# A hybrid decoder layer on one core: the meta tokens' state from one stacked product, two scan outputs in one step, and moving rows placed at the weights' address modulo 256

## The chip, the cores and the metric

The kernel runs on one core of a Trainium2 chip. A core has a matrix engine (TensorE, "PE" in the profile; its weight loads are listed apart as "PEld"), a vector engine (VectorE, "DVE"), an activation engine (ScalarE, "ACT"), a general engine (GpSimd, "POOL") and a queue engine (SyncE, "SP"), each working through its own list of instructions in order, and DMA engines that move data from the chip's main memory. The metric is the device time of one execution in microseconds (us). Three runs of the kernel before gave a median of 1025.13 us, from 1024.91 to 1025.34.

## The reference

One decoder layer works on 512 positions of width 1024, with 16 learned "meta" positions put in front (528 in all; the 16 are dropped at the end). After a normalization, one wide projection makes the inputs of two branches that run side by side, and their gates:

```python
u = rmsnorm(h, mix_norm_w[i])
proj = u @ w_in[i]                      # pool inputs, z, x/B/C, dt, gates
y_pool = pool_mixer(u_pool, pool_w_group[i], pool_scale[i]) @ w_pool_up[i]
y_ssd = mamba2_branch(z, xbc, dt_raw, ...) @ w_ssd_out[i]
h = h + (gate_pool * y_pool + gate_ssd * y_ssd) @ w_o[i]
v = rmsnorm(h, mlp_norm_w[i])
hid = jax.nn.relu(v @ w_ff1[i])
h = h + (hid * hid) @ w_ff2[i]
out = rmsnorm(h, final_norm_w)[:, N_META:]
```

The Mamba-2 branch has 32 heads of width 64 in 8 groups of 4; B and C (128 states) are shared by a group. It runs over chunks: the 16 meta tokens are a partial chunk of their own, and four chunks of 128 follow.

```python
y_diag = einsum(cb * lmat, x*dt)                       # inside a chunk
states = einsum("bclgn,bclgr,bcgrpn", b, decay, x*dt)  # one state per chunk
h_next = chunk_decay * h + states                      # from chunk to chunk
y_off  = einsum(c, h, exp(a_cs))                       # what earlier chunks bring in
y = (y_diag + y_off + x * d_skip) * silu(z)            # then a norm per group
```

The change touches how the meta chunk's state (16 positions, 128 states, 4 heads of 64) is computed, how `y_off` and `y_diag` of the two halves of a group are ordered, and where some operands lie in the on-chip memory.

## The kernel before, in words

**Precision.** Most products run with both factors split in two: `hi` is the float32 number rounded to the matrix engine's faster float32r format, `lo` the rest, and three products (hi·hi, hi·lo, lo·hi) are added up in PSUM. So each weight block of 128 x 1024 is fetched by SP's queue (`raw`, L72), copied to `whi` by ACT (L73), and its rest `wlo` is made by DVE (L74). Some small products are left in plain float32, which the matrix engine takes in two passes (two records in the trace): the chunks' products `pcb`, `pst`, `po` and `py`.

**Projections.** `proj` (L143, L144, L146) walks over eight k-steps. `narrow` projections (z, gates) use moving rows of 512 positions, 24 matmuls a block. `wide` ones (x, B, C, pooled inputs), which also need the meta tokens, move two runs of 258, 260 or 264 positions, 48 matmuls a block. The moving rows are the split `u` (`uh`, `ul`; before the norm is known, `xh`, `xl`), kept as tiles of 64 + 512 floats whose last 528 are used: a narrow slice starts 64 floats into its tile, a wide one 48.

**The scan.** For each group g, `ssd(g)` is a generator of seven steps: transposes (`ptb`, `ptm`, `ptx`) and the decayed inputs (`xdt`, `xdd`; for the meta tokens `xdtm`, `xddm`); then `pcb` and the state products `pst`, the first of them (L449) over the 16 meta tokens, which DVE chains from chunk to chunk (`st`, L455 and L456); then one step for each of the two 128-row halves (`po` at L464, `py` at L470, four DVE instructions); then three steps for the group's norm. `group_proj(g + 1)` is a generator of the next group's projections: `bt` (`px` 16 + g), `ct` (24 + g), two of `xc` (2g, 2g + 1), sometimes a gate, then `pz`. `weave` takes the two in turn, one step of each.

**What sets the order.** Each engine executes a fixed list in order. The lists are not simply the order of the source: when the program is built, a planner orders each engine's list by its own estimate of when inputs are ready, so parts of `po` stand between matmuls of a projection. A wait at the head of a list holds everything behind it on that engine. `px`, `pz` and the like share two PSUM buffers of two banks (`psa`); the scan's tiles share four of one bank (`psb`), so a buffer has to be read out before its second successor can start.

**Later stages**, which the change touches only by where `u` and the pooled rows lie: the pooling branch, the gates, the up-projection, the output projection `w_o` and the MLP, both of the latter with sums of quarter blocks.

Of the kernel before, what the change touches and what calls it, by code (L numbers as in the profile page):

```python
# [9 lines left out]
F32 = mybir.dt.float32  # L10
F32R = mybir.dt.float32r
AF = mybir.ActivationFunctionType
ALU = mybir.AluOpType

P = 128
D = 1024
SEQ = 512
NM = 16
# [3 lines left out]
G = 8  # L22
R = 4
HEADS = 32
DI = 2048
FF = 4096
EPS = 1e-5
# [16 lines left out]

WO_ORDER = [(q, i) for q in ("b11", "b12", "b22") for i in range(2)]
WARM = 9


@with_exitstack
def kernel(ctx: ExitStack, tc, xT, x, w, vec, fnw, out):  # L50
    nc = tc.nc
    act, dve, pe, pool = nc.scalar, nc.vector, nc.tensor, nc.gpsimd
# [45 lines left out]
    ones_f = const.tile([P, P], F32, name="ones_f")  # L98
# [13 lines left out]
    def col(off, i, n=P):  # L112
        return vs[:n, off + i : off + i + 1]

    dtok = const.tile([P, 2, 4, HEADS], F32, name="dtok")
    dtm = const.tile([NM, 2, HEADS], F32, name="dtm")
    dec = const.tile([P, 4, HEADS], F32, name="dec")
    cdec = const.tile([P, 4, HEADS], F32, name="cdec")
    decm = const.tile([NM, HEADS], F32, name="decm")

    u_stack = ExitStack()
    up = u_stack.enter_context(tc.tile_pool(name="up", bufs=1, side="left"))

    up.tile([P, 16], F32, name="u_pad")
    uh = [up.tile([P, 64 + SEQ], F32R, name=f"uh{k}")[:, 64 - NM :] for k in range(NK)]
    ul = [up.tile([P, 64 + SEQ], F32R, name=f"ul{k}")[:, 64 - NM :] for k in range(NK)]

    gc_stack = ExitStack()
    gc = gc_stack.enter_context(tc.tile_pool(name="gc", bufs=2, side="left", reuse_waits="tile"))
    m1p = ctx.enter_context(tc.tile_pool(name="m1p", bufs=1, side="right", reuse_waits="tile"))  # L130
    m1 = [m1p.tile([P, SEQ], F32, tag=f"m1_{d}", name=f"m1_{d}") for d in range(NK)]

# [3 lines left out]
    def psum1(name):  # L136
        return psb.tile([P, 512], F32, tag="s", name=name)
# [25 lines left out]
    pre = pre_stack.enter_context(tc.tile_pool(name="pre", bufs=1, side="right"))  # L163
# [1 line left out]

    xh = [pre.tile([P, 64 + SEQ], F32R, name=f"xh{k}")[:, 64 - NM :] for k in range(NK)]
    xl = [pre.tile([P, 64 + SEQ], F32R, name=f"xl{k}")[:, 64 - NM :] for k in range(NK)]
    pre.tile([P, 24], F32, name="x_pad")
    rsb = pre.tile([P, L], F32, name="rsb")
    q = pre.tile([P, L], F32, name="q")  # L170
    X, U = (xh, xl), (uh, ul)
    H = HEADS

# [7 lines left out]
    b, raw, hi, lo = wdt  # L181
# [3 lines left out]

    for n in range(WARM):
        pe.matmul(pdt[1].rearrange("p (a b) -> p a b", a=4), ones_r,
# [65 lines left out]
    for t, name in ((rsh, "dgh"), (rsl, "dgl")):  # L253
        d = pre.tile([NT, 6, NT], F32R, tag="sq", name=name, bufs=2)
# [3 lines left out]
    for i in range(2):  # L258
        pb = psum1(f"pb1_{i}")
        c = slice(3 * i, 3 * i + 3)  # L260
        for n in range(2):
            pe.matmul(pb[:, : 3 * NT], ones_r[:NT], dg[n][:, c, :].rearrange("p a b -> p (a b)"),
                      start=n == 0, stop=n == 1)
# [11 lines left out]
    for c in range(4):  # L275
        r = slice(c * H, (c + 1) * H)
# [27 lines left out]
    for j, src in enumerate((dt, acs)):  # L304
# [6 lines left out]
              start=True, stop=True)  # L311
# [5 lines left out]
    act.activation(decm, decm, AF.Exp)  # L317
    act.activation(fl(cdec), pq[:, :128], AF.Exp)


    def norm_u():
        for k in range(NK):
            dve.scalar_tensor_tensor(xt[k], xt[k], col(V_MIX, k), rsb, op0=ALU.mult, op1=ALU.mult)
            act.copy(uh[k], xt[k])
            dve.tensor_tensor(ul[k], xt[k], uh[k].bitcast(F32), op=ALU.subtract)
# [54 lines left out]
    def bc(ap, n):  # L380
        return ap.unsqueeze(len(ap.shape)).to_broadcast(list(ap.shape) + [n])

    def ssd(g, cur):

        xc, bt, ct, zt = cur
        hs = slice(R * g, R * g + R)
        tok = lambda c: slice(NM + c * P, NM + (c + 1) * P)
        ctok = lambda c: slice(c * P, (c + 1) * P)
        flat = lambda t: t.rearrange("p r d -> p (r d)")
# [1 line left out]
        nc.gpsimd.dma_start(abc, acs_d[hs, :].partition_broadcast(P))  # L391

        xdt = gs.tile([P, 4, R, 64], F32, tag="xdt", name=f"xdt{g}")
        xdtm = gs.tile([NM, R, 64], F32, tag="xdtm", name=f"xdtm{g}")
        btok = gs.tile([P, 3, P], F32, tag="btok", name=f"btok{g}")
        btm = gs.tile([NM, P], F32, tag="btm", name=f"btm{g}")
        ptb = psum1(f"ptb{g}")
        for c in range(3):
            pe.transpose(ptb[:, c * P : (c + 1) * P], bt[:, tok(c)], ident)
        pe.transpose(ptb[:NM, 3 * P :], bt[:, :NM], ident)  # L400
        act.copy(btok.rearrange("p c n -> p (c n)"), ptb[:, : 3 * P])
        act.copy(btm, ptb[:NM, 3 * P :])
        pm = psum1(f"ptm{g}")
        for i in range(2):
            pe.transpose(pm[:NM, i * P : (i + 1) * P], xc[:, i, :NM], ident)
        dve.tensor_tensor(xdtm, pm[:NM, :256].rearrange("p (r d) -> p r d", r=R),
                          bc(dtm[:, 0, hs], 64), op=ALU.mult)
        for b in range(2):
            pt = psum1(f"ptx{g}_{b}")
            for c in range(2):  # L410
# [4 lines left out]
                              pt.rearrange("p (c r d) -> p c r d", c=2, r=R),  # L415
                              bc(dtok[:, 0, 2 * b : 2 * b + 2, hs], 64), op=ALU.mult)
        xdd = gs.tile([P, 3, R, 64], F32, tag="xdd", name=f"xdd{g}")
        xddm = gs.tile([NM, R, 64], F32, tag="xddm", name=f"xddm{g}")
        dve.tensor_tensor(xddm, xdtm, bc(decm[:, hs], 64), op=ALU.mult)
        dve.tensor_tensor(xdd, xdt[:, :3, :, :], bc(dec[:, :3, hs], 64), op=ALU.mult)  # L420

        eb = gs.tile([P, 2, SEQ], F32, tag="eb", name=f"eb{g}")
# [23 lines left out]
        st = [gs.tile([P, R, 64], F32, tag=f"st{c}", name=f"st{c}_{g}") for c in range(4)]  # L446
        pss = [psum1(f"pst{g}_{b}") for b in range(2)]
        pv = [pss[c // 2][:, (c % 2) * 256 : (c % 2) * 256 + 256] for c in range(4)]
        pe.matmul(pv[0], btm, flat(xddm), start=True, stop=True)  # L449
        for c in range(3):  # L450
            pe.matmul(pv[c + 1], btok[:, c, :], xdd[:, c, :, :].rearrange("p r d -> p (r d)"),
                      start=True, stop=True)
# [5 lines left out]
        yield  # L458

        yt = gs.tile([P, 2, SEQ], F32, tag="yt", name=f"yt{g}")  # L460
        for i in range(2):
            po = psum1(f"po{g}_{i}")
            for c in range(4):
                pe.matmul(po[:, c * P : (c + 1) * P],  # L464
                          flat(st[c])[:, i * P : (i + 1) * P], ct[:, ctok(c)], start=True, stop=True)
            py = psum1(f"py{g}_{i}")
            for c in range(4):
                for j in range(2):
                    r = 2 * i + j
                    pe.matmul(py[64 * j : 64 * j + 64, c * P : (c + 1) * P],  # L470
                              xdt[:, c, r, :], dm[:, r, c, :], start=True, stop=True)
            y = yt[:, i, :]
            dve.tensor_tensor(y, po, eb[:, i, :], op=ALU.mult)
            dve.tensor_tensor(y, y, py, op=ALU.add)
            dve.scalar_tensor_tensor(y, xc[:, i, NM:], col(V_DS, 2 * g + i), y,
                                     op0=ALU.mult, op1=ALU.add)
            dve.tensor_tensor(y, y, zt[:, i, :], op=ALU.mult)
            yield

        sq = gs.tile([P, 2, SEQ], F32, tag="eb", name=f"sqg{g}")  # L480
        act.activation(sq, yt, AF.Square)
# [11 lines left out]
        for i in range(2):  # L493
            y = yt[:, i, :]
# [34 lines left out]
    gs = gc_stack.enter_context(tc.tile_pool(name="gs", bufs=1, side="left", reuse_waits="tile"))  # L529
# [32 lines left out]
    for g in range(G):  # L562
        nxt = group_tiles(g + 1) if g + 1 < G else None
        fill = [group_proj(g + 1, nxt, GATE_AT.get(g))] if nxt else [out_part()]
        if g == 4:
            fill = [out_half()] + fill
        weave(ssd(g, cur), fill, 2 if g == 4 else 1)
        cur = nxt
# [160 lines left out]
    for n, d in enumerate(MERGE):  # L729
# [8 lines left out]
        for i, k in enumerate(ks):  # L738
            c = slice(k * P, (k + 1) * P)
# [294 lines left out]
    c = NC - 1  # L1034
# [5 lines left out]
    for t in range(4):  # L1040
        T, st = t // 2, slice((t % 2) * P, (t % 2 + 1) * P)
        n = 0
        for half in range(2):
            parts = [(0, 512)] if half == 0 or t < 3 else [(0, 256), (256, 256)]
            for a, m in parts:
# [3 lines left out]
                i = 0  # L1049
                for k, seg in ((1, (A11, 3)[T]), (0, (A12, A22)[T])):  # L1050
                    wh, wl = wq[k, half]
                    for p in range(2):
                        x0 = p * 512 + a
                        f = i == 0 and not (T == 0 and half == 0)
                        i += 1
                        for lhs, rhs in ((hh, wh), (hh, wl), (hl, wh)):
                            pe.matmul(ps, lhs[:, p, seg, st], rhs[:, x0 : x0 + m], start=f and lhs is hh and rhs is wh,
                                      stop=i == 4 and lhs is hl, skip_group_check=True)
# [148 lines left out]
```

## Time and profile before

| | |
|---|---|
| median of three runs | 1025.13 us (1024.91 to 1025.34) |
| span of the profiled execution | 1023.3 us |
| the profiled execution's time less the median of the runs | 1023.3 - 1025.13 = -1.8 us: the runs' time holds that much outside the span |
| PE busy | 1014.6 us, 99% of the span |
| DVE, ACT, POOL busy | 730.3, 552.5, 88.7 us |
| granted TensorE clock | 0.999 of full |
| HBM traffic | 102 GB/s over the span |

The profiled execution has no time of its own beside its span; what lies outside the span is taken as the 1.8 us of the table. The page gives busy time by engine, the chain of work that ended last, and groups of instructions by line. A matmul's record overlaps its successors' (its end is modelled), so the distance from one start to the next is what a matmul costs the engine; the timeline shows the starts. A float32 product has two records.

### The profile page before, as it was taken

What the parts mean: (1) busy time and instruction counts of PE and PEld (TensorE: products, weight loads), DVE (VectorE), ACT (ScalarE), POOL (GpSimd) and SP (SyncE); (2) the same over time, 40 slices, a digit from 0 to 9 for tenths busy, and PEclk for the clock granted to TensorE, in tenths of its full rate; (3) what the DMA queues carried; (4) which work ended last, traced back from release to release, by engine and by line L of the source; (5) the groups of instructions that cost most, each with busy time, mean ns of one, the idle gap of its engine ahead of it and who ended that gap; (6) DMA issues with size and microseconds to landing.
All of it is one profiled execution on the core that took longest, in us unless ns stands there. A gap on an engine that the chain in (4) does not pass through costs nothing.

```text
span 1023.3 us, 14063 instructions
## 1 busy us (share of the span) xinstructions
PE 1014.6 (99%) x5697; PEld 876.7 (86%) x5697; DVE 730.3 (71%) x954; ACT 552.5 (54%) x728; POOL 88.7 (9%) x52
## 2 busy tenths in 40 slices
PE   9999999999999999999999999999999999999997
PEld 8889989998879898988899888888888888888886
DVE  7978788687746586978755457975777577666866
ACT  7775968586627339573244343474545355454444
POOL 0100000000000000000000001003040421413400
PEclk9999999999999999999999999999999999999999
DMA  7243051414332331414532333224323323334112
GB/s 237 72 160 103 21 166 38 148 46 141 102 101 86 103 104 42 145 41 141 189 102 84 103 104 120 86 91 156 103 69 122 120 83 113 95 102 124 42 42 83
DMA packets 29281, 105.63 MB, mean 103 GB/s; under 512 B 3296, under 2 KB 4256, under 8 KB 28192
## 3 DMA queue, kind: packets, MB, share of 16 engines
q1 hardware_dynamic: 26496, 92.75, 28.7%
q0 software_dynamic: 2000, 11.08, 3.0%
q8 instruction: 45, 0.74, 0.3%
q10 hardware_dynamic: 720, 0.91, 0.3%
q14 instruction: 20, 0.16, 0.1%
HBM read 102.55 MB, written 2.16 MB: 102 GB/s over the span
## 4 chain that ended last, share of the span: by engine, by line
PE 96%; DVE 2%; ACT 0%; DMA 0%; issue 0%; SPq 0%; ACTq 0%
PE px L143 6%; PE px L144 6%; PE pf L92 6%; PE pf L91 6%; PE px L146 6%; PE pf L90 6%; PE alpha L956 3%; PE alpha L957 3%; PE alpha L958 3%; PE pz L143 3%; PE pz L146 3%; PE pz L144 3%; PE py L470 2%; PE pso L90 2%; PE pp L144 2%; PE pp L146 2%
## 5 line engine op out<-in xcount | busy, mean ns | idle before, releaser
L73 ACT CAST whi<-raw 128x1024 fp32r<-128x1024 f32 (+1 forms) x131 | 135.7, 1043 | 220.0 <-PE pf L91 55.8
L74 DVE TENSOR_TENSOR wlo<-raw,whi 128x1024 fp32r<-128x1024 f32 (+1 forms) x131 | 163.6, 1251 | 112.6 <-ACT whi L73 105.3
L143 PE MATMUL px<-uh,whi 128*128 128x264 f32 (+1 forms) x448 | 121.2, 290 | 0.7 <-DVE ct L334 0.7
L144 PE MATMUL px<-ul,whi 128*128 128x264 f32 (+1 forms) x448 | 118.9, 285 | 0.0
L90 PE MATMUL pf<-vh,whi 128*128 128x512 f32 x256 | 99.8, 390 | 0.0
L92 PE MATMUL pf<-vh,wlo 128*128 128x512 f32 x256 | 99.6, 389 | 0.0
L91 PE MATMUL pf<-vl,whi 128*128 128x512 f32 x256 | 99.6, 389 | 0.0
L146 PE MATMUL px<-uh,wlo 128*128 128x264 f32 (+1 forms) x448 | 90.8, 284 | 0.0
L143 PEld LDWEIGHTS px<-uh,whi 128*128 128x128 f32 x448 | 84.6, 189 | 2.8 <-issue 2.6
L144 PEld LDWEIGHTS px<-ul,whi 128*128 128x128 f32 x448 | 84.8, 189 | 0.3
L718 DVE TENSOR_TENSOR slo<-b,shi 128x1024 fp32r<-128x1024 f32 x35 | 49.1, 1403 | 31.6 <-ACT shi L717 31.6
L146 PEld LDWEIGHTS px<-uh,wlo 128*128 128x128 f32 x448 | 69.4, 188 | 0.3 <-issue 0.3
L717 ACT CAST shi<-b 128x1024 fp32r<-128x1024 f32 x35 | 36.8, 1050 | 47.2 <-PE pf L91 36.4
L91 PEld LDWEIGHTS pf<-vl,whi 128*128 128x128 f32 x256 | 48.1, 188 | 10.0
L90 PEld LDWEIGHTS pf<-vh,whi 128*128 128x128 f32 x256 | 48.1, 188 | 9.9
L92 PEld LDWEIGHTS pf<-vh,wlo 128*128 128x128 f32 x256 | 48.1, 188 | 9.9
L967 POOL TENSOR_TENSOR b<-b,b 128x1024 f32<-128x1024 f32 x14 | 35.7, 2548 | 238.3 <-DVE slo L718 238.3
L956 PE MATMUL alpha<-shi,hh 128*128 128x512 f32 x140 | 54.6, 390 | 0.0
L957 PE MATMUL alpha<-slo,hh 128*128 128x512 f32 x140 | 54.5, 389 | 0.0
L958 PE MATMUL alpha<-shi,hl 128*128 128x512 f32 x140 | 54.5, 389 | 0.0
L783 DVE TENSOR_TENSOR ht<-ht,alpha 128x1024 f32<-128x1024 f32 x35 | 42.5, 1214 | 10.9 <-PE alpha L958 10.9
L143 PE MATMUL pz<-uh,whi 128*128 128x512 f32 x112 | 44.0, 393 | 0.0
(412 smaller groups left out, 2513.7 us busy)
## 6 DMA issues: line engine op xcount, KB each, us to landing
raw<-in_w SPq DMA_DIRECT2D x129, 512.0 KB, 3.6
b<-in_w SPq DMA_DIRECT2D x28, 512.0 KB, 3.6
abc<-acs_d POOLq DMA_DIRECT2D x8, 1024.0 KB, 7.2
wob<-in_w SPq DMA_DIRECT2D x8, 512.0 KB, 4.6
xt<-in_xT SPq DMA_DIRECT2D x8, 264.0 KB, 5.6
ht<-in_x POOLq DMA_DIRECT2D x4, 512.0 KB, 6.7
w<-in_w SPq DMA_DIRECT2D x4, 512.0 KB, 3.6
out_dram<-out SPq DMA_DIRECT2D x4, 320.0 KB, 2.4
```

The lines of the kernel that those rows point to most:

```text
L73: act.copy(hi[:, c], raw[:, c])
L74: dve.tensor_tensor(lo[:, c], raw[:, c], hi[:, c].bitcast(F32), op=ALU.subtract)
L90: pe.matmul(ps, ah, bh, start=first, stop=False)
L91: pe.matmul(ps, ah, bl, start=False, stop=False)
L92: pe.matmul(ps, al, bh, start=False, stop=last)
L143: pe.matmul(o, wh, rhs[0][k][:, c], start=k == 0, stop=False)
L144: pe.matmul(o, wh, rhs[1][k][:, c], start=False, stop=False)
L146: pe.matmul(o, wl, rhs[0][k][:, c], start=False, stop=k == NK - 1)
L718: dve.tensor_tensor(lo, src, hi.bitcast(F32), op=ALU.subtract)
L956: pe.matmul(ps[t], a[0], wh[:, cs], start=f, stop=False, skip_group_check=True)
L957: pe.matmul(ps[t], a[0], wl[:, cs], start=False, stop=False, skip_group_check=True)
L958: pe.matmul(ps[t], a[1], wh[:, cs], start=False, stop=l, skip_group_check=True)
```

## The change

Three edits are made together.

1. The meta tokens' state. Before, DVE made `xdtm` (x times dt) and `xddm` (times the decay), and one float32 product of 16 rows (`btm` by `xddm`) gave the state. Now dt is multiplied into the decay once for all heads, `xdm` is made in one DVE instruction, and three parts are stacked on 80 rows of two tiles that are zeroed once: `bm` holds B's hi part at rows 0 to 15 and 32 to 47 and its rest at 64 to 79, `xm` holds x's hi part at rows 0 to 15 and 64 to 79 and its rest at 32 to 47. One float32r product over 80 rows adds the three. In each group ACT makes four copies where it made one, and DVE two subtractions where it made one product. `bm` and `xm` have one buffer each.
2. Both scan tiles in one step. The products `po` of both halves come first, then `py` of both, then DVE's four instructions for each; `ssd` has six steps, one fewer.
3. Places. The 64-byte pad ahead of `uh` is gone, the pad behind `xl` grows by 64 bytes. In the built programs `uh`, `ul`, `xh`, `xl` and the pooled rows `ph`, `pl` start at 32 modulo 256 before and at 224 after; `whi` and `wlo` start at 224 in both.

```diff
-    up.tile([P, 16], F32, name="u_pad")
...
+    bm = gc.tile([MQ, P], F32R, name="bm", bufs=1)
+    xm = gc.tile([MQ, R, HEAD], F32R, name="xm", bufs=1)
+    dve.tensor_scalar(bm, ones_f[:MQ], 0.0, None, op0=ALU.mult)
...
-    pre.tile([P, 24], F32, name="x_pad")
+    pre.tile([P, 40], F32, name="x_pad")
...
+    dve.tensor_tensor(decm, dtm[:, 0, :], decm, op=ALU.mult)
...
-        act.copy(btm, ptb[:NM, 3 * P :])
+        hi, mid, low = slice(0, NM), slice(32, 32 + NM), slice(64, 64 + NM)
+        pbm = ptb[:NM, 3 * P :]
+        act.copy(bm[hi], pbm)
+        act.copy(bm[mid], pbm)
+        dve.tensor_tensor(bm[low], pbm, bm[hi].bitcast(F32), op=ALU.subtract)
...
-        dve.tensor_tensor(xdtm, pm[:NM, :256].rearrange("p (r d) -> p r d", r=R),
-                          bc(dtm[:, 0, hs], 64), op=ALU.mult)
+        dve.tensor_tensor(xdm, pm[:NM, :256].rearrange("p (r d) -> p r d", r=R),
+                          bc(decm[:, hs], 64), op=ALU.mult)
+        act.copy(xm[hi], xdm)
+        act.copy(xm[low], xdm)
+        dve.tensor_tensor(xm[mid], xdm, xm[hi].bitcast(F32), op=ALU.subtract)
...
-        dve.tensor_tensor(xddm, xdtm, bc(decm[:, hs], 64), op=ALU.mult)
...
-        pe.matmul(pv[0], btm, flat(xddm), start=True, stop=True)
+        pe.matmul(pv[0], bm, flat(xm), start=True, stop=True)
...
+        po = [psum1(f"po{g}_{i}") for i in range(2)]
+        py = [psum1(f"py{g}_{i}") for i in range(2)]
         for i in range(2):
-            po = psum1(f"po{g}_{i}")
             for c in range(4):
-                pe.matmul(po[:, c * P : (c + 1) * P],
+                pe.matmul(po[i][:, c * P : (c + 1) * P],
...
+        for i in range(2):
             y = yt[:, i, :]
-            dve.tensor_tensor(y, po, eb[:, i, :], op=ALU.mult)
-            dve.tensor_tensor(y, y, py, op=ALU.add)
+            dve.tensor_tensor(y, po[i], eb[:, i, :], op=ALU.mult)
+            dve.tensor_tensor(y, y, py[i], op=ALU.add)
...
-            yield
+        yield
```

More of the change, by code (lines that the diff above doesn't have):

```diff
@@ L24 @@
 HEADS = 32
+HEAD = 64
 DI = 2048
@@ L46 @@
 WARM = 9
+MQ = 80
 @with_exitstack
@@ L129 @@
     gc = gc_stack.enter_context(tc.tile_pool(name="gc", bufs=2, side="left", reuse_waits="tile"))
+    bm = gc.tile([MQ, P], F32R, name="bm", bufs=1)
+    xm = gc.tile([MQ, R, HEAD], F32R, name="xm", bufs=1)
+    dve.tensor_scalar(bm, ones_f[:MQ], 0.0, None, op0=ALU.mult)
+    for i in range(2):
+        dve.tensor_scalar(xm[:, 2 * i : 2 * i + 2, :].rearrange("p r d -> p (r d)"), ones_f[:MQ], 0.0, None,
+                          op0=ALU.mult)
     m1p = ctx.enter_context(tc.tile_pool(name="m1p", bufs=1, side="right", reuse_waits="tile"))
@@ L393, in ssd @@
         xdt = gs.tile([P, 4, R, 64], F32, tag="xdt", name=f"xdt{g}")
-        xdtm = gs.tile([NM, R, 64], F32, tag="xdtm", name=f"xdtm{g}")
+        xdm = gs.tile([NM, R, 64], F32, tag="xdm", name=f"xdm{g}")
         btok = gs.tile([P, 3, P], F32, tag="btok", name=f"btok{g}")
-        btm = gs.tile([NM, P], F32, tag="btm", name=f"btm{g}")
         ptb = psum1(f"ptb{g}")
@@ L417, in ssd @@
         xdd = gs.tile([P, 3, R, 64], F32, tag="xdd", name=f"xdd{g}")
-        xddm = gs.tile([NM, R, 64], F32, tag="xddm", name=f"xddm{g}")
-        dve.tensor_tensor(xddm, xdtm, bc(decm[:, hs], 64), op=ALU.mult)
         dve.tensor_tensor(xdd, xdt[:, :3, :, :], bc(dec[:, :3, hs], 64), op=ALU.mult)
@@ L460, in ssd @@
         yt = gs.tile([P, 2, SEQ], F32, tag="yt", name=f"yt{g}")
+        po = [psum1(f"po{g}_{i}") for i in range(2)]
+        py = [psum1(f"py{g}_{i}") for i in range(2)]
         for i in range(2):
-            po = psum1(f"po{g}_{i}")
             for c in range(4):
-                pe.matmul(po[:, c * P : (c + 1) * P],
+                pe.matmul(po[i][:, c * P : (c + 1) * P],
                           flat(st[c])[:, i * P : (i + 1) * P], ct[:, ctok(c)], start=True, stop=True)
-            py = psum1(f"py{g}_{i}")
+        for i in range(2):
             for c in range(4):
@@ L469, in ssd @@
                     r = 2 * i + j
-                    pe.matmul(py[64 * j : 64 * j + 64, c * P : (c + 1) * P],
+                    pe.matmul(py[i][64 * j : 64 * j + 64, c * P : (c + 1) * P],
                               xdt[:, c, r, :], dm[:, r, c, :], start=True, stop=True)
+        for i in range(2):
             y = yt[:, i, :]
-            dve.tensor_tensor(y, po, eb[:, i, :], op=ALU.mult)
-            dve.tensor_tensor(y, y, py, op=ALU.add)
+            dve.tensor_tensor(y, po[i], eb[:, i, :], op=ALU.mult)
+            dve.tensor_tensor(y, y, py[i], op=ALU.add)
             dve.scalar_tensor_tensor(y, xc[:, i, NM:], col(V_DS, 2 * g + i), y,
```

## The prediction

> **What bounds the kernel now.** I read the page first (busy time, the chain that ended last), then the clock by core, then the timeline of PE and DVE around one group's scan. A timeline row gives start, duration, engine, line, operation, tiles, shape and count, and in brackets the idle time before it.
>
> ```profile
> PE 1014.6 (99%) x5697; PEld 876.7 (86%) x5697; DVE 730.3 (71%) x954; ACT 552.5 (54%) x728; POOL 88.7 (9%) x52
> ...
> PE 96%; DVE 2%; ACT 0%; DMA 0%; issue 0%; SPq 0%; ACTq 0%
> ```
>
> ```profile
> core 0: 1023.3 us, clock 0.999
> ```
>
> PE is busy 99% of the span at full clock and carries 96% of the chain. So the time is PE's own list plus whatever makes its head wait. An instruction less on PE counts in full; work on DVE and ACT costs nothing until PE waits for it, and then it counts in full too, since nothing behind gives slack back.
>
> Group 3's scan, PE's timeline, then DVE's:
>
> ```profile
> 210.94 0.38 PE L405 MATMUL ptm<-ident,xc 128*16 128x128 f32 x2
> 211.16 1.04 PE L413 MATMUL ptx<-ident,xc 128*128 128x128 f32 x8
> 211.95 0.37 PE L143 MATMUL px<-uh,whi 128*128 128x264 f32 x1
> ...
> 217.90 1.06 PE L442 MATMUL pcb<-ct,bt 128*128 128x128 f32 x8
> 218.89 0.69 PE L449 MATMUL pst<-xddm,btm 16*128 16x256 f32 x2
> 219.51 1.56 PE L451 MATMUL pst<-xdd,btok 128*128 128x256 f32 x6
> 220.72 0.47 PE L143 MATMUL px<-uh,whi 128*128 128x258 f32 x1
> ```
>
> ```profile
> 211.36 0.41 DVE L406 TENSOR_TENSOR xdtm<-ptm,dtm 16x256 f32<-16x256 f32 x1 [0.42 <-PE ptm L405]
> 211.80 1.29 DVE L414 TENSOR_TENSOR xdt<-ptx,dtok 128x512 f32<-128x512 f32 x2
> 213.00 0.40 DVE L419 TENSOR_TENSOR xddm<-xdtm,decm 16x256 f32<-16x256 f32 x1
> ...
> 214.54 0.94 DVE L420 TENSOR_TENSOR xdd<-xdt,dec 128x768 f32<-128x768 f32 x1
> ...
> 216.00 1.21 DVE L74 TENSOR_TENSOR wlo<-raw,whi 128x1024 fp32r<-128x1024 f32 x1
> 219.00 0.69 DVE L444 TENSOR_TENSOR cbm<-pcb,tri 128x512 f32<-128x512 f32 x1 [1.79 <-PE pcb L442]
> 219.79 2.29 DVE L457 TENSOR_TENSOR abc<-abc,cbm 128x2048 f32<-128x2048 f32 x1
> 222.00 0.76 DVE L334 SCALAR_TENSOR_TENSOR bt<-px,vs,bt 128x527 f32<-128x527 f32 x1
> 222.68 0.41 DVE L455 TENSOR_TENSOR st<-st,cdec 128x256 f32<-128x256 f32 x1
> ```
>
> Between the transposes and `pcb` stands a whole `px` block, 211.95 to 217.90. In these 6 us DVE makes all that `pst` needs (`xdd` ends at 215.5, 3.4 us before `pst`) and `wlo` for the next block. That cover is the point of the case. A queued DVE instruction starts before the last one's record ends (the tap of `bt` ends at 222.76, `st` starts at 222.68), so I take each at its duration less 0.08.
>
> **Part 1, the meta product.** `pcb`'s eight records span 1.06, the last 0.28 long: 0.11 from start to start. So the last starts at 217.90 + 7 x 0.11 = 218.67, and from there to the first `xdd` product at 219.51 are 0.84, of which 0.11 are `pcb`'s own: the 16-row product costs 0.73. The new one has 80 rows and one float32r record of 256 columns. Nearest rows, an 88-row product and 128-row ones (`px`) among float32 ones:
>
> ```profile
> L262 PE MATMUL pb<-dgh,ones_r x2: 287/288/288, 24.7 to 24.8; 88*128 88x264 f32 x2
> ```
>
> ```profile
> 126.50 0.60 PE L464 MATMUL po<-ct,st 128*128 128x128 f32 x4
> 127.03 1.09 PE L470 MATMUL py<-abc,xdt 128*64 128x128 f32 x16
> 128.06 0.39 PE L143 MATMUL px<-uh,whi 128*128 128x264 f32 x1
> 128.28 0.29 PE L144 MATMUL px<-ul,whi 128*128 128x264 f32 x1
> ...
> 128.53 0.28 PE L144 MATMUL px<-ul,whi 128*128 128x264 f32 x1
> 128.65 1.05 PE L464 MATMUL po<-ct,st 128*128 128x128 f32 x8
> 130.39 0.36 PE L143 MATMUL px<-uh,whi 128*128 128x264 f32 x1 [0.68 <-DVE ct L334]
> ```
>
> 88 rows run as a full product does (a record of 288 ns, against 280 to 290 for 128 rows), where the two of 16 rows span 0.69. A `px` matmul costs 0.12 (128.53 to 128.65), the first after plain float32 0.22: 0.10 for the turn. So 0.22 for 0.73, 0.51 to 0.6 a group (0.1 more if the first `xdd` product, now after a full-height one, loses its slow start): 0.55 x 8 = **-4.4**. Bounds: 0 if 80 rows behaved as 16, -4.8. DVE's and ACT's added instructions are priced below, where PE waits. The three zeroings stand third in DVE's list, where DVE sits idle until the first weights are split:
>
> ```profile
> 4.41 0.42 DVE L200 TENSOR_TENSOR wlo<-raw,whi 128x256 fp32r<-128x256 f32 x1 [2.96 <-ACT whi L199]
> ```
>
> At no more than `xddm`'s 0.40 each, twice as wide, they fit into those 2.96 us; without that cover they would cost up to 1.2. So 0.
>
> **Part 2, the order.** I read the built lists of both kernels against each other. From plain float32 (`pcb`, `po`, `py`) PE turns into a projection 29 times before, 21 times after; it enters `py` 21 times, then 16. A turn costs 0.10; entering `py` costs 0.53 - 4 x 0.11 = 0.09 (126.50 to 127.03). 8 x 0.10 + 5 x 0.09 = **-1.2**. The one step also holds all four one-bank PSUM buffers with `po` and `py` until DVE has read them; the next to want one is `png`, and a whole `px` block of 6 us (as at 211.95) stands before it, so I price that at 0; without the block it would cost the rest of DVE's eight instructions.
>
> But the lists show more. In groups 3, 4 and 6 the changed PE list has no block between the transposes and `pcb`: `ptm`, seven `ptx`, `pcb`, `pst` follow `pz` directly, and the block (`px`, in group 4 `pso`) comes behind. DVE's list there is `xdm`, two `xdt`, `cbm`, `xdd`, and only then `xm`'s middle part, which needs ACT's copy, queued behind `zt`'s activation; the next `whi` and `wlo` stand behind all of it.
> - DVE from `ptm`'s end (0): 0.04, `xdm` 0.33, the two `xdt` 1.20 (211.80 to 213.00), `cbm` 0.61, 0.1 and `xdd` 0.87, the middle part 0.40 (taken as `xddm`): 3.55. PE meanwhile: seven transposes 0.69, `pcb` 0.9, less the 0.17 by which `ptm`'s record outlasts its turn: 1.4. Wait: 3.55 + 0.05 - 1.4 = 2.2, three times: **+6.6**.
> - Behind that DVE has `abc` (2.29, for which ACT's second exponential comes about 0.2 late) and `wlo` (1.21), 3.6 in all; PE has the products (0.22 + 1.2), four matmuls each of two blocks (0.6 + 0.6) and a `po` pair (0.45), 3.1. Wait 0.5, and 0.2 for `whi`: 0.7 in groups 3 and 6; in group 4, where two `pso` blocks start at once and both want `whi` and `wlo`, 1.2. **+2.6**.
> - Group 1: the third `px` (4) needs the PSUM buffer of the first (18), which DVE frees with `bt`'s third tap. The changed DVE list is `cbm`, tap, `abc`, tap, `st`, tap, with the `wlo` of block 26 behind, so PE cannot run block 26 meanwhile. From the end of block 18: `pcb` 1.1, `cbm` 0.69, tap 0.7, `abc` 2.2, tap 0.7, `st` 0.33, tap 0.7: 6.4. PE: `pcb` 0.9, `pst` 1.4, four matmuls 0.6, `po` 0.45: 3.4. **+3.0**. The 0.68 at 130.39, the same wait one block later, goes: **-0.7**.
> - Group 7, where block `psp` wants a `wlo` behind `abc` (2.29) and `st`, 0.8; group 0, `po` behind a tap, 0.2: **+1.0**.
>
> Waits together: 6.6 + 2.6 + 3.0 - 0.7 + 1.0 = **+12.5**. Ends: 0.08 more or less for each of some 35 queued instructions on DVE and ACT, 9.7 to 15.3. SP's and POOL's lists keep their order but for two loads.
>
> **Part 3, the places.** One block of 24 narrow matmuls from `u`, then one of the output projection, whose moving rows already lie at 224 modulo 256:
>
> ```profile
> 607.04 0.40 PE L143 MATMUL pgs<-uh,whi 128*128 128x512 f32 x1
> ...
> 612.32 0.39 PE L146 MATMUL pgs<-uh,wlo 128*128 128x512 f32 x1
> ...
> 645.48 0.39 PE L771 MATMUL wo_alpha<-shi,a1h 128*128 128x512 f32 x1
> ...
> 650.92 0.39 PE L771 MATMUL wo_q<-shi,sah 128*128 128x512 f32 x1
> ```
>
> `pgs`: 612.32 - 607.04 = 5.28 over 23 steps, 229.6 ns each. `wo`: 650.92 - 645.48 = 5.44 over 24, 226.7. So 2.9 ns at most by place; narrow blocks and pooled products hold 849 such matmuls: -2.5 at most, nothing at least if the difference is not the place. Taken: 2.5 ns, **-2.1**. The wide matmuls (some 1,890) shift by the same 64 bytes, but from 0 to 56 bytes past the weights' place to 192 to 248 past it, for which no row exists: between -2.9 and +2.9 ns each, -5.5 to +5.5 us; I take 0, since the wide rows of before already lie off the weights' place for the most part and the shift moves them from one such place to another.
>
> The rows give a cost to the place. [...]
>
> **The sum.** -4.4 - 1.2 + 12.5 - 2.1 + 0 = +4.8 on the profiled 1023.3 us; the median is 1.8 above the span, so 1025.1 + 4.8 = **1029.9**.
>
> **The rivals.**
> - *Wide rows worse*: the new place costs all 1,890 up to 2.9 ns: 1029.9 + 5.5 = 1035.4. Nothing in the trace excludes it. 0.13.
> - *Wide rows better*: the mirror image, 1024.4, no measurable change. 0.12.
> - *The place does nothing*: 1025.1 + 6.9 = 1032.0. Against it 229.6 and 226.7; for it that the two blocks differ in more than place. 0.10.
> - *Faster, by waits that do not appear*: PE's gain is 7.7. If in groups 3, 4 and 6 the middle part of `xm` were ready when `pcb` ends, because DVE's list runs ahead of my estimate, the 6.6 and the 2.6 behind it would go: 1029.9 - 9.2 = 1020.7. It decides once the waits fall under 5.7. Against it, `xdd`'s 0.94 and two `xdt` cannot start before the transposes. 0.12.
> - *80 rows as slow as 16*: 1034.3, part of the upper end. 0.03.
>
> Forecast 0.50. 0.2% (about 2 us) is what a measurement can tell from no change: below 1023.1 faster, above 1027.2 slower. Faster: 0.12 and a part of the better wide rows. Same: the rest of those and the low flank of the forecast. That gives 0.13, 0.14, 0.73. The range reaches from the better wide rows with slightly shorter waits, 1022, to the worse ones, 1036; the forecast's own is 1026 to 1033.
>
> **What would show it.** PE idle of about 2 us before `pst` in groups 3, 4 and 6, ended by DVE's middle part; about 3 us before block 4 in group 1; a `pgs` step of 227 ns; an 80-row record of about 0.29 us. Wrong if PE's idle time there is under 6 us together, or if a wide step moves by more than 2 ns.

## The result and the profile after

The changed kernel takes 1039.21 us (median of four runs, 1037.43 to 1039.89), against 1025.04 for the kernel before beside it: a ratio of 1.0134, with an interval from 1.0120 to 1.0149. It is 14.2 us slower. The forecast was 1029.9, in a range up to 1036: the direction was right, the size was not.

The profiled execution took 1037.43 us, 1035.7 of them in its span. From the page of the changed kernel, its busy line, the shares of the chain that ended last, and its clock:

```profile
PE 1011.8 (98%) x5689; PEld 875.4 (85%) x5689; DVE 737.1 (71%) x966; ACT 565.2 (55%) x756; POOL 88.6 (9%) x52
...
PE 84%; ACT 9%; DVE 4%; issue 2%; DMA 0%; DVEq 0%; ACTq 0%
```

```profile
core 0: 1035.7 us, clock 0.996
```

PE is busy for 2.8 us less (1011.8 for 1014.6). The prediction had it save 7.7; the two can't be set against each other directly, since records overlap and part of the time ran at a lower clock, 0.996 for 0.999. The chain that was 96% PE is now 84%, and ACT, which had nothing of it, carries 9%, DVE 4%. So PE waits. The chain follows each wait back through the list that made it long, and there ACT has more than DVE. The sums that follow name only what came last before PE went on, and there DVE has more (total us, times, the longest):

```profile
PE pst L462 <- DVE xm L422: 6.6, 3, 2.2
PE px L150 <- ACT whi L75: 3.0, 2, 1.5
PE px L150 <- DVE bt L343: 2.7, 1, 2.7
...
PE px L153 <- DVE wlo L76: 1.1, 2, 0.6
```

Here is group 3's scan, the stretch that the prediction showed of the kernel before: PE's timeline, then DVE's, then ACT's. Lines are those of the changed kernel: 420 to 422 make `xm`, 449 and 450 are the two exponentials of `abc`, 385 is `zt`.

```profile
212.40 0.27 PE L417 MATMUL ptm<-ident,xc 128*16 128x128 f32 x1
212.51 0.93 PE L428 MATMUL ptx<-ident,xc 128*128 128x128 f32 x7
213.27 1.06 PE L455 MATMUL pcb<-ct,bt 128*128 128x128 f32 x8
216.51 0.36 PE L462 MATMUL pst<-xm,bm 80*128 80x256 f32 x1 [2.19 <-DVE xm L422]
216.71 1.46 PE L464 MATMUL pst<-xdd,btok 128*128 128x256 f32 x6
219.66 0.39 PE L150 MATMUL px<-uh,whi 128*128 128x264 f32 x1 [1.49 <-ACT whi L75]
...
221.33 0.28 PE L151 MATMUL px<-ul,whi 128*128 128x258 f32 x1
222.18 0.51 PE L153 MATMUL px<-uh,wlo 128*128 128x264 f32 x2 [0.57 <-DVE wlo L76]
```

```profile
214.97 0.95 DVE L433 TENSOR_TENSOR xdd<-xdt,dec 128x768 f32<-128x768 f32 x1
215.95 0.41 DVE L422 TENSOR_TENSOR xm<-xdm,xm 16x256 fp32r<-16x256 f32 x1
218.70 2.29 DVE L470 TENSOR_TENSOR abc<-abc,cbm 128x2048 f32<-128x2048 f32 x1 [2.33 <-ACT abc L449]
```

```profile
212.19 1.06 ACT L450 ACTIVATE abc<-abc 128x1024 f32<-128x1024 f32 x1
213.27 1.28 ACT L385 ACT_TABLE_LOAD   x1
214.56 1.02 ACT L385 ACTIVATE zt<-pz 128x1024 f32<-128x1024 f32 x1
215.49 0.39 ACT L420 CAST xm<-xdm 16x256 fp32r<-16x256 f32 x1
215.90 0.40 ACT L421 CAST xm<-xdm 16x256 fp32r<-16x256 f32 x1
216.32 1.28 ACT L449 ACT_TABLE_LOAD   x1
217.61 1.06 ACT L449 ACTIVATE abc<-abc 128x1024 f32<-128x1024 f32 x1
218.57 1.03 ACT L75 CAST whi<-raw 128x1024 fp32r<-128x1024 f32 x1
```

The projection block that stood between the transposes and `pcb` is gone, as the prediction read from the lists. `pcb`'s eight records are issued by 213.27 + 8 x 0.11 = 214.15, and `pst` starts at 216.51: 2.36 us lost. That was foreseen. What was not foreseen stands behind it. The six `xdd` products take 1.21 (as they did before, 219.51 to 220.72), so the next block could start at 217.92. It starts at 219.66, 1.74 late, when ACT has made its `whi`. ACT has no idle moment in this list: the first exponential, a table load, `zt`, `xm`'s two copies, another table load, the second exponential, and only then `whi`. DVE, which the prediction took for the limit, sits idle for 2.33 us before `abc`, until that second exponential is there. `wlo` follows `abc`, so it is late too: the next wait is 0.57 by the row.

In the kernel before, ACT's list for the same group stood otherwise:

```profile
211.64 1.03 ACT L376 ACTIVATE zt<-pz 128x1024 f32<-128x1024 f32 x1
...
214.72 1.03 ACT L73 CAST whi<-raw 128x1024 fp32r<-128x1024 f32 x1
215.76 1.28 ACT L436 ACT_TABLE_LOAD   x1
217.06 1.06 ACT L436 ACTIVATE abc<-abc 128x1024 f32<-128x1024 f32 x1
218.02 1.04 ACT L437 ACTIVATE abc<-abc 128x1024 f32<-128x1024 f32 x1
```

There `zt` comes ahead of both exponentials, one load of 1.28 us serves the two, and `whi` is made before them, by 215.75, 5 us before PE wants it at 220.72. In the changed kernel `zt` stands between the two exponentials, so the second has a load of its own (at 216.32), and `whi` comes last. Over the whole execution ACT makes four loads more (58 before, 62 after); what weighs here is where they stand.

The clock is the second thing not foreseen. PE's granted clock in five stretches of 3.41 us of the changed kernel (the columns are the window, its length, the busy time and count of PE, PEld, DVE, ACT and POOL, the clock, the DMA share and GB/s):

```profile
119.83:123.24 3.41, 0.86 (x8) 0.66 (x6) 3.41 (x5) 1.77 (x2) 0.00 (x0) 1.00 0.00 0
123.24:126.65 3.41, 3.28 (x18) 2.95 (x18) 3.41 (x6) 1.93 (x2) 0.00 (x0) 0.50 0.21 35
266.59:270.00 3.41, 1.22 (x11) 1.03 (x10) 2.76 (x5) 3.36 (x5) 0.00 (x0) 1.00 0.00 0
270.00:273.41 3.41, 2.95 (x8) 1.79 (x6) 1.63 (x1) 3.40 (x4) 0.00 (x0) 0.50 0.00 0
409.93:413.34 3.41, 1.65 (x7) 1.17 (x7) 1.02 (x3) 3.36 (x5) 0.00 (x0) 1.00 0.00 0
```

Twice the clock is halved for 3.41 us, once behind group 1's wait and once behind group 4's; in the kernel before it is full from start to end of this part. The two stretches lie 146.76 us apart, and a 43rd of that is 3.413: they fit one grid in time. Each follows a grid window in which PE was busy for little (0.86 and 1.22 us); behind the window with 1.65 busy, the least of all the others, nothing happens. So a window need not be idle throughout to have half clock behind it.

### The profile page after: what moved, and what is told of

Read it like the earlier page. It is cut to its first block, busy times and chain, and to the rows that moved or that the text cites. A ratio compares the mean times of both kernels' runs of the same rounds, so it can differ in the third digit from the quotient of the medians.

```text
span 1035.7 us, 14112 instructions
## 1 busy us (share of the span) xinstructions
PE 1011.8 (98%) x5689; PEld 875.4 (85%) x5689; DVE 737.1 (71%) x966; ACT 565.2 (55%) x756; POOL 88.6 (9%) x52
## 4 chain that ended last, share of the span: by engine, by line
PE 84%; ACT 9%; DVE 4%; issue 2%; DMA 0%; DVEq 0%; ACTq 0%
PE pf L93 6%; PE pf L92 6%; PE pf L94 6%; PE px L150 5%; PE px L153 5%; PE px L151 5%; PE alpha L971 3%; PE alpha L972 3%; PE alpha L973 3%; PE py L484 2%; PE pz L153 2%; PE pz L150 2%; PE pz L151 2%; PE pp L153 1%; PE pp L151 1%
```

## The experiments

The theory at this point: the scan's missing step takes the projection block out of groups 3, 4 and 6; PE then waits first for DVE's list and then for ACT's with its table loads; and the idle windows halve the clock. The rivals: the places (the wide rows lie worse), the stacked product with its chain of copies, or the new order of the products itself.

**One part at a time.** First the places alone.

```diff
-    up.tile([P, 16], F32, name="u_pad")
...
-    pre.tile([P, 24], F32, name="x_pad")
+    pre.tile([P, 40], F32, name="x_pad")
```

> Edit 3 alone: the moving rows of u, x and the pooled products move to the weights' place modulo 256, nothing else changes. Theory (the lost time is PE's waits, and the places only gain): the order of every engine's list stays, 849 narrow matmuls gain 2.5 ns each, the wide ones nothing: 1025.0 - 2.1 = 1022.9, between 1022 and 1024. Rival (the wide rows lie worse at their new place and carry part of the 14 us): 1026 to 1030.6, with wide steps up to 2.9 ns longer than before.

Measured: 1021.97 us (1021.58 to 1022.82), ratio 0.9968, interval 0.9955 to 0.9980: 3.3 us faster. The block of `pgs` that the prediction used, first and last of its 24 matmuls:

```profile
593.20 0.39 PE L142 MATMUL pgs<-uh,whi 128*128 128x512 f32 x1
...
598.41 0.39 PE L145 MATMUL pgs<-uh,wlo 128*128 128x512 f32 x1
```

(598.41 - 593.20) / 23 = 226.5 ns a step, for 229.6 before: the narrow rows gained what was said, 2.1 to 2.6 us over 849 of them. The other 0.7 to 1.2 is not from them. The wide rows gained a little as well: group 3's `px` block, which took 5.95 us from `px` to `pcb` (211.95 to 217.90), now takes 5.90:

```profile
210.85 0.37 PE L142 MATMUL px<-uh,whi 128*128 128x264 f32 x1
...
216.75 1.05 PE L441 MATMUL pcb<-ct,bt 128*128 128x128 f32 x8
```

That is 1 ns a step over 48 steps; if all 1,890 wide matmuls gain it, some 2 us (an estimate from this one block), which is more than enough. So the rival with worse wide rows falls, and so does the one by which places do nothing: the edit moves nothing but addresses.

Then the stacked product alone.

```diff
-        pe.matmul(pv[0], btm, flat(xddm), start=True, stop=True)
+        pe.matmul(pv[0], bm, flat(xm), start=True, stop=True)
```

(with the tiles, the copies and the subtractions that it needs, as in the change)

> Edit 1 alone: the stacked product of 80 rows, with seven steps of the scan as before. Theory (the waits come from the scan having one step less, not from the new product): PE's products save about 4.4 us, the projection block stays between the transposes and pcb in every group, and pst never waits 2 us; shorter products uncover smaller waits elsewhere, about 5 us in all, so 1024 to 1027. Rival (the chain of three copies and subtractions ahead of the product, xdm to ACT to DVE, costs its 2.3 us wherever it stands): three to eight waits of 2 us before pst, 1030 to 1038.

Measured: 1026.13 us (1025.97 to 1028.94), ratio 1.0016, interval 1.0007 to 1.0025: 0.8 us slower. No 2 us wait stands before `pst` in groups 3, 4 and 6. But PE's saved time is gone all the same: it arrives earlier and waits for others, 1.4 us before `pst` in group 7, and 1.0 us each for `ct` in group 1 and for a `whi` in group 2. The longest, 1.5 us before `py` in group 2, has no releaser in the profile. In the profiled run the two waits of group 2 halve the clock once, from 174.4 to 177.8 us.

Then the one step alone, with the 16-row product and the old places.

```diff
+        po = [psum1(f"po{g}_{i}") for i in range(2)]
+        py = [psum1(f"py{g}_{i}") for i in range(2)]
...
-            yield
+        yield
```

> Edit 2 alone: both halves of the scan's products in one step, six steps, with the 16-row product and the old places. Theory (one step less moves the projection block out from between the transposes and pcb): pst waits in three or four groups for the products' inputs although no stacked operand exists, and the next block waits for whi behind it; 1025.0 + 8 to 13 = 1033 to 1038. Rival (the stacked product's chain makes the waits): only the fewer turns show, 1024.

Measured: 1034.32 us (1033.71 to 1035.50), ratio 1.0090, interval 1.0075 to 1.0105: 9.0 us slower. So most of the loss needs neither the stacked product nor the places. The waits stand in groups 2, 3, 4 and 6: half a microsecond before `pst`, for `xddm`, and then up to 1.5 us for `whi` behind it.

**Is it the order of the products or the number of steps?** Edit 2 does both: it orders `po`, `po`, `py`, `py`, and it makes seven steps six. The next kernel is the one before with a step less and nothing else.

```diff
             dve.tensor_tensor(y, y, zt[:, i, :], op=ALU.mult)
-            yield
+        yield
```

> The kernel before with nothing changed but one step of the scan fewer: the products stay in their old order (po, py of one half, then of the other), the 16-row product and the old places stay. Theory (the number of steps alone moves the projection block): most of edit 2's loss appears without its new order of the products, + 5 to + 9: 1030 to 1034. Rival (the new order of the products, with all four one-bank buffers held, is what costs): no change, 1025.

Measured: 1034.26 us (1033.25 to 1034.91), ratio 1.0088, interval 1.0073 to 1.0103: as much as edit 2, and 0.3 above the upper edge expected. PE in group 4:

```profile
264.89 0.67 PE L449 MATMUL pst<-xddm,btm 16*128 16x256 f32 x2 [0.47 <-DVE xddm L419]
265.67 1.56 PE L451 MATMUL pst<-xdd,btok 128*128 128x256 f32 x6
268.52 0.50 PE L90 MATMUL pso<-yh,whi 128*128 128x512 f32 x1 [1.29 <-ACT whi L73]
```

Without a stacked product, at the old places, with the products in their old order, the same two waits appear, one for DVE and a longer one for ACT. The rival falls: the number of steps is what costs. And the other way round: all three edits, with one empty step put back.

```diff
         dve.tensor_tensor(dm, dm, cbm.unsqueeze(1).to_broadcast([P, R, 4, P]), op=ALU.mult)
         yield
+        yield
```

> All three edits, and one empty step of the scan between the state products and the scan products, so that the scan has seven steps again. Nothing is computed otherwise. Theory (the number of steps sets the order): the projection block stands again between transposes and pcb in groups 3, 4 and 6, the waits of 2.3 us and those behind them go, 12 us less than with the three edits: 1023 to 1026. Rival (both halves' products in a row, with all four one-bank buffers held, or the stacked product, make the waits): 1034 or more.

Measured: 1023.42 us (1022.47 to 1023.86), ratio 0.9981, interval 0.9972 to 0.9990. One line that computes nothing is worth 15.8 us and turns a loss into a gain. PE in group 3:

```profile
212.86 1.04 PE L428 MATMUL ptx<-ident,xc 128*128 128x128 f32 x8
213.65 0.37 PE L150 MATMUL px<-uh,whi 128*128 128x264 f32 x1
...
219.55 1.05 PE L455 MATMUL pcb<-ct,bt 128*128 128x128 f32 x8
220.36 0.36 PE L462 MATMUL pst<-xm,bm 80*128 80x256 f32 x1
220.56 0.81 PE L464 MATMUL pst<-xdd,btok 128*128 128x256 f32 x3
```

The block is back between the transposes and `pcb`, 213.65 to 219.55, and `pst` follows without a wait. These rows also price the stacked product: 220.56 - 220.36 = 0.20 us, where the prediction said 0.22.

**Is it ACT?** The next kernel leaves out the silu of the gate in groups 3, 4 and 6 and takes an identity in its place, for which group 3's rows below show no table load.

```diff
-            act.activation(zf, ps, AF.Silu)
+            act.activation(zf, ps, AF.Identity if g in (3, 4, 6) else AF.Silu)
```

> All three edits, and in groups 3, 4 and 6 the gate zt goes through an identity in place of silu (so its values are left wrong there), which needs no table load: in the profile with the three edits ACT makes two loads of 1.28 us each around it, just ahead of xm's copies and of whi. Theory (ACT's queue with its table loads holds xm's parts and the next whi): the wait before pst falls by about 0.3 to 0.9 (what is left is DVE's own list), the 1.5 for whi goes, 7 us less in the three groups, and perhaps a stretch of half clock less: 1037.4 - 7 = 1030, down to 1028. Rival (DVE's list is the limit, as in the prediction, and ACT's lag is without weight): 1037 to 1040 as with the three edits.

Measured: 1031.95 us (1029.75 to 1034.23), 7.3 us less than with the three edits. The profiled run, the shortest, is where it was expected; the median is 2 us above, and the three longer runs have a clock of 0.991 to 0.996 for 0.998. ACT in group 3, then PE:

```profile
211.91 1.06 ACT L450 ACTIVATE abc<-abc 128x1024 f32<-128x1024 f32 x1
212.88 1.01 ACT L385 ACTIVATE zt<-pz 128x1024 f32<-128x1024 f32 x1
...
214.62 1.06 ACT L449 ACTIVATE abc<-abc 128x1024 f32<-128x1024 f32 x1
215.58 1.03 ACT L75 CAST whi<-raw 128x1024 fp32r<-128x1024 f32 x1
```

```profile
215.33 0.35 PE L462 MATMUL pst<-xm,bm 80*128 80x256 f32 x1 [1.32 <-DVE xm L422]
216.23 1.13 PE L464 MATMUL pst<-xdd,btok 128*128 128x256 f32 x4 [0.54 <-DVE xdd L433]
217.01 0.47 PE L150 MATMUL px<-uh,whi 128*128 128x264 f32 x1
```

From the first exponential's start to `whi`'s are 3.67 us, for 6.38 with the loads: two loads of 1.28 and some 0.15 by which neighbours now overlap. The wait for `whi` is gone in all three groups. The wait before `pst`, now split in two, only falls from 2.19 to 1.32 + 0.54 as the rows give it: most of that one is DVE's own, as the prediction had it. So both lists hold PE, one behind the other. Two things moved along with the loads. The planner ordered the lists anew (DVE makes `xm`'s part ahead of `xdd`, and PE takes four `px` matmuls between the `xdd` products), so the split of the first wait is not the loads' alone. And in the profiled run no stretch at half clock is left, group 1's among them, which the edit does not touch. From `ptm` to the first product with `wlo`, group 3 takes 7.49 us (212.08 to 219.57) for 9.78 with the loads (212.40 to 222.18); groups 4 and 6 gain 2.5 and 2.3, the three together 7.2.

**Is the half clock PE's idleness?** Products that nobody reads are put where PE idles.

```diff
+        for n in range(2 if g in (3, 4, 6) else 0):
+            for c in range(4):
+                pe.matmul(pss[0][:, c * P : (c + 1) * P], bt[:, tok(c)], ct[:, ctok(c)], start=True, stop=True)
...
+        for n in range(3 if g == 1 else 0):
+            for c in range(4):
+                pe.matmul(po[0][:, c * P : (c + 1) * P], bt[:, tok(c)], ct[:, ctok(c)], start=True, stop=True)
```

> All three edits, and products that nobody reads put on PE just where it idles: eight more of pcb's kind ahead of pst in groups 3, 4 and 6 (some 1.8 us each, in a wait of 2.35), twelve ahead of po in group 1 (2.7 us, in a wait of 2.8). Theory (PE's clock is halved for 3.41 us after a stretch of 3.41 us in which PE idled for some 2.3 us or more): no half clock is left in groups 1 and 4 and, although PE has 8 us more work, the time falls by about 1.7 for each stretch: 1034 to 1036. Rival (the halving has another cause than PE's idleness): 1037 to 1040, with the stretches at half clock still there; or, if the waits are not waits of PE, 8 us more, 1045.

Measured: 1037.78 us (1037.27 to 1039.13), 1.4 us less than without them although PE has some 8 us more to do (the ranges of the two overlap), but not the 1034 to 1036 expected. The time lies where the rival put it, so the windows have to tell:

```profile
118.00:130.00 12.00, 11.86 (x96) 10.90 (x95) 10.40 (x14) 5.75 (x8) 0.00 (x0) 1.00 0.31 94
215.84:219.25 3.41, 1.48 (x10) 1.01 (x9) 2.02 (x1) 3.40 (x6) 0.00 (x0) 1.00 0.00 0
219.25:222.66 3.41, 3.31 (x15) 2.88 (x14) 3.41 (x6) 1.04 (x2) 0.00 (x0) 0.50 0.30 48
```

Group 1's half clock is gone. But in group 3 the wait for `whi` now lies wholly inside one window of the grid (1.48 us busy), and the clock is halved behind it where it was not before; group 4 keeps its stretch too. So the expectation missed by its count of windows. The cleaner test is a kernel in which one wait of more than 2 us is left. That is all three edits with the empty step in groups 1 to 7 only (the long one is group 1's; the next longest, 1.9 us, is before `pst`):

```diff
+        if g in (1, 2, 3, 4, 5, 6, 7):
+            yield
```

> All three edits, and the empty step in groups 1 to 7 only, not in group 0. Theory (the alignment of the two lists sets the waits): as with the empty step everywhere, without the waits of group 2 (about 3 us) and with group 1's wait of 3 us for a PSUM buffer back: 1021 to 1023, of which 1.7 are a stretch at half clock if group 1's wait falls into one window. Rival (the measured gain of the empty step is not due to alignment): 1025 or more.

Measured: 1020.69 us (1019.28 to 1022.32), ratio 0.9957, interval 0.9942 to 0.9971. The profiled run is the longest, with half clock from 123.05 to 129.88; the two shortest runs, 1019.28 and 1019.65, have a mean clock of 0.999 and 1.000, the longest 0.995. Then the same kernel with group 1's twelve unread products:

> As the empty step in groups 1 to 7, with twelve products that nobody reads ahead of po in group 1, in its wait of 2.8 us for a PSUM buffer, the only wait left that is long enough to halve the clock (the profile without them shows half clock from 123.05 to 129.88). Theory (the half clock follows PE's idleness): no stretch at half clock is left, 1.7 to 3.4 us less than the profiled run, 1017 to 1019, and the runs lie closer together than the 3 us of the kernel without them. Rival (it has another cause): 1020 to 1022 and a stretch at half clock as before; if the products came on top of the wait, 1023.

Measured: 1019.70 us (1019.35 to 1020.55), ratio 0.9949, interval 0.9935 to 0.9962. The same 12 us of both, without the products and then with them:

```profile
118.00:130.00 12.00, 9.18 (x49) 7.96 (x48) 10.92 (x15) 6.79 (x9) 0.00 (x0) 0.72 0.28 85
```

```profile
118.00:130.00 12.00, 11.86 (x96) 10.90 (x95) 10.40 (x14) 6.10 (x8) 0.00 (x0) 1.00 0.31 87
```

The clock rises from 0.72 to 1.00 and the spread of the runs falls from 3.0 to 1.2 us. The median lies 0.7 above the upper edge expected, at the level of the runs that had no half clock anyway: filling a wait buys back the clock, nothing more. These are one trace of each, and two of the four runs without the products had a mean clock of 0.999 and 1.000 too, so the pair alone does not settle it. Two things speak for it beside the pair. In the kernel with all the waits filled, too, group 1's stretch is gone. And when the traces of twelve of the thirteen kernels (all but the one with edits 1 and 2 together) are cut on the grid, seven times the clock is halved ahead of the span's last 5 us, six of them behind a window with 0.86 to 1.48 us of PE busy, and no window with less than 1.5 goes by without it. So the rival, another cause than PE's idleness, has little left; the seventh case stands with the open points at the end.

**Do the edits add?** Alone they gave -3.3, +0.8 and +9.0, which adds up to +6.5; in one kernel they cost 14.2. All but the places:

```diff
+    up.tile([P, 16], F32, name="u_pad")
...
-    pre.tile([P, 40], F32, name="x_pad")
+    pre.tile([P, 24], F32, name="x_pad")
```

> Edits 1 and 2 together, the old places. Alone they gave +0.8 and +9.0, which would make 1035. Theory (edit 2 takes the block away and edit 1 makes the chain behind it longer, so their costs do not add: the wait before pst is 2.3 us in three groups instead of 0.8, and long enough to halve the clock; the places are worth 3.3 us beside it): 1039.2 + 3.3 = 1042.5, between 1040.5 and 1044. Rival (the edits add, and the places lose their gain, or cost, beside the waits): 1035 to 1039.

Measured: 1042.13 us (1039.08 to 1043.53), ratio 1.0157, interval 1.0140 to 1.0174. The places are worth about 3 us here too. Edits 1 and 2 together cost 17.0, not 9.8. The trace shows two parts of the difference: once the block is gone, the stacked product's longer chain lies open (2.2 us of wait before `pst` in three groups, for 0.5 with edit 2 alone), and more of it runs at a lower clock (a mean of 0.992 in the profiled run, for 0.996 with all three edits; behind group 3's wait the row of the six `xdd` products, at 218.87, is 2.75 us long, for 1.46). How much each is worth was not separated.

**A version that beats both.** All three edits, with the scan of groups 1 and 7 in its old order and seven steps, and the empty step in groups 2 to 6.

```diff
+        if g in (2, 3, 4, 5, 6):
+            yield
...
+        if g in (1, 7):
+            for i in range(2):
+                po = psum1(f"po{g}_{i}")
...
```

> All three edits, but the scan of groups 1 and 7 in its old order and seven steps, and the empty step in groups 2 to 6. Theory (waits and half clock are what is left to win): group 1's wait of 2.8 us becomes two of 1.5 and 0.7, too short to halve the clock, and group 7's wait behind po (0.8) goes or halves: 1017 to 1019, at or below the kernel with the products that nobody reads. Rival (both halves in one step is itself worth something in those groups): 1020 or more.

Measured: 1019.44 us (1018.16 to 1020.55), ratio 0.9942, interval 0.9929 to 0.9954: 5.9 us faster than the kernel before and 19.8 us faster than the changed one, with no unread products. That is 0.4 above the upper edge expected, and 0.6 below the rival's 1020. Group 1's wait is split into 1.2 and 0.6, and the clock is full there; group 7's wait of 2.2 before `pst` is the longest that is left.

## Why the prediction was wrong, step by step

- **Part 1, PE's side: right.** 0.20 us for the 80-row product, against 0.22 forecast. (Its record is 0.36 long, where the prediction named 0.29; what counts is the distance to the next start.)
- **The block that goes in groups 3, 4 and 6, and DVE's list before `pst`: right.** 2.36 us in group 3, forecast 2.2; three waits, 6.6 in the list of waits as in the sum. Group 1: 123.37 less 120.53 is 2.84, forecast 3.0; the old wait of 0.68 is gone, as forecast.
- **The step that failed: "Behind that ... Wait 0.5, and 0.2 for `whi`: 0.7 in groups 3 and 6; in group 4 ... 1.2. +2.6".** It walked DVE's list and took ACT to be nearly free ("ACT's second exponential comes about 0.2 late"). The exponential came 2.33 late. In group 3 the waits behind `pst` are 1.74 and 222.18 - 221.45 = 0.73, 2.5 together; group 6 has the same (1.77 and 0.72), group 4 some 2.9. Together 7.9 for 2.6. The cause is ACT's list, with two table loads of 1.28 us in it, one on each side of `zt` between the two exponentials, and `whi` behind them all: the prediction allowed 0.08 a queued instruction, and names no load. The run without loads takes the wait for `whi` away and shows it to be ACT's.
- **A term that was missing: the half clock.** Group 1's stretch costs, by estimate, half of its 3.28 busy us, 1.6: a `px` step there takes 0.22 us (123.72 to 123.94), for 0.12 at full clock (127.12 to 127.24). Group 4's lies for the most part under the wait for ACT: the block behind `pst` starts 7.29 us after `ptm` there (265.45 to 272.74), and 7.26 and 7.29 after it in groups 3 and 6, which had full clock. What it costs beyond that is in the 2.9 above. No row of the profile before showed a halved clock in the middle of the span, and none showed PE idle for 2 us either. The range's upper end came from the places, and none of the rivals was a longer wait.
- **Groups 7 and 0: too small.** `po` in group 0 lost 0.57 for 0.2, `psp` in group 7 about 1.1 for 0.8 (it starts at 465.72 and could at 464.61).
- **Part 3: right for the narrow rows, a little more with the wide ones**, 3.3 us for 2.1. A wide step moved by 1 ns where the prediction took 0 and allowed 2.9. The rivals on both sides of it, with a quarter of the chance, were about the term that mattered least.

The sum, mended: waits 7.1 + 7.9 + 2.8 + 1.6 - 0.7 + 1.7 = 20.4 for 12.5, places -3.3 for -2.1. That makes 1029.9 + 7.9 - 1.2 = 1036.6; the profiled run took 1037.4. The median is 1.8 above that run. The other runs show a mean clock of 0.993 to 0.996, so a further stretch at half clock fits some of them, but there is no trace of them. So of the 9.3 us that the forecast was short, 6.7 are found and 2.6 stay open.

Part 2's gain from fewer turns (1.2) could not be told from the rest: edit 2 alone and the dropped step alone cost the same within 0.1 us, where the first should have been 1.2 less; the trace was not taken apart for it.

## What to carry to other kernels

Where a planner orders the lists, an edit's price lies in the order that comes out: here one generator step fewer cost 9 us, and an empty one brought it back with interest. When a cover goes, walk every engine that stands behind the wait to the end of its own list, table loads at full length (1.28 us each here) included; the engine that ends the first wait need not be the one that ends the second. And edits that are cheap under a cover may not be added up once it is gone.

## What was not expected of the hardware

- In these traces PE's clock is halved for a window of 3.41 us after a window in which PE was little busy: 0.86 to 1.48 us in six cases, while one with 1.65 (the changed kernel, 409.93 to 413.34) went by without it. The windows of the changed kernel fit one grid to the end: its last half clock starts at 1034.6, 267 times 3.413 behind 123.24. One case does not fit: with a step less, half clock from 411.64 us stands behind a window with 1.91 busy, so the recorded busy time does not decide it alone. The same wait costs nothing more, or an estimated 1.6 us more, by where it falls on the grid: group 1's is 2.68 us in the changed kernel, with half clock behind it; without table loads PE is idle there all of 122 to 124 us, but a border of the grid lies within, at 123.4 (264 windows ahead of the half clock at that trace's end, from 1024.52), and the clock stays full. Runs of one kernel then differ by up to 4.5 us, as those without the places do, where 21 runs of the kernel before differ by 1.0. Why the clock stayed halved for two windows behind group 1 with the step in groups 1 to 7 (123.05 to 129.88), though PE was busy for 2.9 us in the first of them, is open.
- In group 3 of the changed kernel a table load of 1.28 us starts when the instruction ahead of it has ended (213.25 and 213.27) and holds the next one to its end (214.55 and 214.56), while `zt` and the copy behind it overlap by 0.09, the second exponential and `whi` by 0.10.
- Moving the moving rows by 64 bytes, to the weights' address modulo 256, is worth 3 ns of a matmul with 512 columns (229.6 before, 226.5 after, one block of `pgs`) and 1 ns of a wide one (5.95 and 5.90 us for 48 steps, so 124 and 123 ns, one `px` block). Whether the distance to the weights counts, or the address by itself, no run here tells: only this one pair of places was measured.
